# Two-layer attention and pooling trunk: buffers for the operand preparation, one more projection in block form, two clearings on ScalarE

## The chip, the cores and the metric

One core of a Trainium2 chip runs the whole program. The metric is the device time of one execution in microseconds (us), median of three runs. The engines of the core each work through their own queue in order: TensorE (PE in the profile, with its weight loads as PEld), VectorE (DVE), ScalarE (ACT), GpSimd (POOL) and SyncE (SP), which here only starts DMAs.

## The reference

A sequence of 512 tokens of 1024 channels goes through an attention layer, a feed-forward layer, a pooling layer and a second feed-forward layer. Only the attention is touched by the change:

```python
h = rmsnorm(x, attn_norm)                              # 512 x 1024
qkv = (h @ w_qkv).reshape(B, S, 3, 3, 8, 128)          # 3 groups, q/k/v, 8 heads
for g, (window, dil) in enumerate(((128, 1), (512, 4), (2048, 16))):
    outs[g], lses[g] = dilated_window_attention(q[g], k[g], v[g], window, dil, slopes[g])
o = sum(softmax(lses) * outs)                          # merged over the groups
x = x + o.reshape(512, 1024) @ w_out
```

So each of the 8 heads needs a q and a k projection in each of 3 groups (six products of 1024x128 weights with the 1024x512 normalized input), and values.

## The kernel before

**Products.** Every float32 operand is held as a high and a low part (`split`: ScalarE copies to the rounded type, VectorE subtracts), and each product takes three matmuls: high by high, high by low, low by high. A plain projection (`Product`) has 8 pieces of 128 channels, 24 matmuls of 512 columns. A pair of projections, q and k of one group, can instead be done in block form (`seven`): seven half-size products instead of eight, 84 matmuls of 256 columns, with sums of operand blocks prepared on VectorE. Head 0 is done plainly; so are the first `NSOLO = 3` groups of head 1, which is all of that head; from head 2 on all pairs go through `seven`.

**Operand preparation.** The block form needs the normalized input and its block sums. `prepare(k)` makes them for channel pieces k and k+4, for k = 0 to 3: `normed` writes the normalized pieces to one buffer h (L574, two instructions of 512 columns) and the block sums to a buffer t (L578, L579, L583), and four `split` calls (ACT L91, DVE L92) turn them into the tiles that the matmuls read (`near`, `h`, `tx`). Before, h and t are taken from the ring `raw` of four buffers, into which the weights are loaded by DMA before they are split.

**Weights.** `loads` and `steps` are queues of weight transfers and weight splits. `pump` is called behind each product and issues what has free buffers: `raw` (4), `rawhalf` (2), `w` (5), `half` (2). A plain projection takes one `raw`. A block-form pair (`Pair`) takes two `raw` and one `rawhalf`, its second buffer gets an accumulating DMA from GpSimd's queue (L172), and two additions on VectorE (L188, L189) make its third matrix.

**Order.** The Python code gives instructions in program order, and a scheduler of the framework then sets the order of each engine's queue, by its own estimate of when operands are ready. What stands in a queue is therefore not the order of the code.

**Steps around the change**, in the order of TensorE's queue:

- head 0: six plain projections, two plain value products; between them `scores0(0)` (L712), `scores12(0)` (L732, L736) and `turn_values(0)`, whose eight transposes (L685) read the two tiles `vt` that VectorE evacuates (L606): four transposes for the first tile, four for the second;
- head 1: six plain projections, evacuated by L606 to the tiles `qk`. Behind the first group's pair stands `merge(0)`: its first instruction is a matmul (L765) of `far`, which `scatter` writes on VectorE (L753) from the maxima and sums `st` of head 0. These come from `scores12(0)`: L739 and L742, L743 on VectorE, then four exponentials with their sums on ScalarE (L746). Behind the third group stand `turn0(0)` and `turn12(0)` (transposes L795, L816), then `scores0(1)` (L712);
- `values12` (L628 to L630) and, from there on, block form for everything of the attention.

`turn0` and `turn12` clear their tiles `t0` and `t12` once, by a memset on VectorE (L791, L812). These tiles lie in the room of `late` and `late12`, parts of the operand that the plain projections read.

Of the kernel before, what the change touches and what calls it, by code (L numbers as in the profile page):

```python
# [8 lines left out]
F32 = mybir.dt.float32  # L9
F32R = mybir.dt.float32r  # L10
AF = mybir.ActivationFunctionType
# [4 lines left out]
P = 128  # L16
S = 512
# [7 lines left out]
NT = S // P  # L25
# [13 lines left out]
K2 = KC // 2  # L39
NPLAIN = 4  # L40
WARM = 5
NSOLO = 3
PARTS = ((0, 2, False), (2, 10, True), (10, 18, True), (18, 22, False))
ENDS = 5
BACK = {"blocks": 3, "sums": 7}
# [19 lines left out]
def trunk(ctx: ExitStack, tc: tile.TileContext, xT, xN, norms, w_first, w_qk, w_qkp, w_v0, w_v0p, w_v12, w_out, w_pair, w_down, w_dblock, w_pin, w_pgrp,  # L65
          consts, ident_in, invcnt_in, outT, outR):
    nc = tc.nc
# [5 lines left out]
    def x_tile(k, name="x", dtype=F32):  # L73
        return cpool.tile([P, S], dtype, tag=f"x{k}", name=name)
# [4 lines left out]
    ones = cpool.tile([P, 1], F32, name="ones")  # L79
    nhalf = cpool.tile([P, NT], F32, name="nhalf")  # L80

    def ps():
        return psum.tile([P, S], F32, tag="ps", name="ps")
# [6 lines left out]
    def split(hi, lo, v):  # L90
        nc.scalar.activation(hi, v, AF.Copy)  # L91
        nc.vector.tensor_tensor(lo, v, hi.bitcast(F32), op=OP.subtract)  # L92
# [7 lines left out]
    class Held:  # L100


        def __init__(self, ring, shift=0):
            self.live = True
            n = COLS[ring]
            if ring in ("w", "half"):
                t = wpool.tile([P, 2 * n + LINE], F32R, tag=ring, name=ring, bufs=BUFS[ring])
                self.t = [t[:, shift + i * n:shift + (i + 1) * n] for i in range(2)]
            else:
                self.t = wpool.tile([P, n], F32, tag=ring, name=ring, bufs=BUFS[ring])  # L110
            rings[ring].append(self)
# [106 lines left out]
    def pairs(*srcs, shift=LINE // 4, back=False):  # L218

        these = [Pair(src, shift, back) for src in srcs]  # L220
        for parts in zip(*(p.steps() for p in these)):
            steps.extend(parts)
        units.append((these,))
# [11 lines left out]
    def plain(*srcs, lean=False):  # L235
        for src in srcs:
            share(1, src, lean=lean)

    for h in range(HEADS):
        if h == 0:  # L240
            plain(*[w_qk[u] for u in range(len(QK) - NF)])
        for g in range(3):
            if h == 1 and g < NSOLO:
                plain(*[w_qk[len(QK) - NF + 2 * g + c] for c in range(2)])
            elif h:
                pairs(w_qkp[3 * h - 3 - NSOLO + g])
        if h == 0:
# [86 lines left out]
    room, taken = {}, {}  # L334
# [36 lines left out]
    def product(layer):  # L371
        return Product(KC, stream(layer)).add(range(KC)).p
# [59 lines left out]
    def finish(lead, layer, ks):  # L432

        for f in lead:
            f.add(ks)
        r = rstd([acc[layer]])
        lead += begin(1, layer, range(4))
        row = row_of(spread(r))
        lead[-1].add(range(4, KC))
        return row  # L440
# [129 lines left out]
    def normed(layer, k, row, h, t, chained=False):  # L570

        for i in range(2):
            c = k + i * K2
            nc.vector.scalar_tensor_tensor(h.t[:, i * S:(i + 1) * S], X[c], nrm[:, layer, c:c + 1], row,  # L574
                                           op0=OP.mult, op1=OP.mult)
        hq = h.t.rearrange("p (a b c) -> p a b c", a=2, b=2)
        tq = t.t.rearrange("p (a b c) -> p a b c", a=2, b=2)
        nc.vector.tensor_sub(tq[:, :, 0], hq[:, :, 1], hq[:, 0])  # L578
        nc.vector.tensor_sub(t.t[:, H2:S], t.t[:, :H2], h.t[:, 3 * H2:])  # L579
        if chained:  # L580
            nc.vector.scalar_tensor_tensor(t.t[:, 3 * H2:], t.t[:, H2:S], -1.0, h.t[:, S:3 * H2], op0=OP.mult, op1=OP.subtract)
        else:
            nc.vector.tensor_add(t.t[:, 3 * H2:], t.t[:, H2:S], h.t[:, S:3 * H2])  # L583
        return h, t

    def halves_of(hi, lo):
        return [tuple(v[:, a * H2:(a + 1) * H2] for v in (hi, lo)) for a in range(2)]
# [8 lines left out]
    with tc.tile_pool(name="opool", bufs=1) as opool:  # L596
        early = opool.tile([P, HEADS, S], F32R, tag="o", name="early")
        with tc.tile_pool(name="apool", bufs=1) as apool:
            const = apool.tile([P, 5 * P], F32, name="const")
            d0, d12, swap = const[:, :2 * G], (const[:, 2 * G:2 * G + P], const[:, 2 * G + P:3 * G]), const[:, 3 * G:3 * G + P]  # L600
            rows = {}
# [87 lines left out]
            def blk(t, b, n=1):  # L689
                return t[:, b * P:(b + n) * P]  # L690
# [66 lines left out]
            def merge(h):  # L757
# [22 lines left out]
                for r in range(NT):  # L780
                    v = s12[:, r]
                    nc.scalar.activation(v, v, AF.Copy, scale=co[:, 1, r:r + 1])

            T0 = []

            def turn0(h):

                s0 = A[h]["s0"]
                if not T0:
                    T0.append(apool.tile([P, 2 * NT - 1, P], F32, name="t0"))  # L790
                    nc.vector.memset(T0[0], 0.0)  # L791
                own, before = T0[0][:, :NT], T0[0][:, NT:]
                p = ps()
                for b in range(NT):
                    nc.tensor.transpose(blk(p, b), s0[:, b, :P], ident)  # L795
                pb = p.rearrange("p (b q) -> p b q", b=NT)
                for j in range(NT):
                    c = slice(j * NI, (j + 1) * NI)
                    nc.scalar.copy(before[c, :, :c.stop], pb[c, 1:, :c.stop])
                    if j < NT - 1:  # L800
                        nc.scalar.copy(own[c, :, c.stop:], pb[c, :, c.stop:])
                    nc.vector.transpose(own[c, :, c], s0[c, :, P:])
                A[h]["t0"] = own, before

            T12 = []

            def turn12(h):

                s12 = A[h]["s12"]
                if not T12:  # L810
                    T12.append(apool.tile([P, 2, NT, P], F32, name="t12"))
                    nc.vector.memset(T12[0][:, 1], 0.0)  # L812
                t12 = T12[0]
                p = ps()
                for r in range(NT):
                    nc.tensor.transpose(blk(p, r), s12[:, r, :P], ident)  # L816
                nc.scalar.copy(t12[:, 0].rearrange("p r k -> p (r k)"), p)

                for j in range(NT):
                    c = slice(j * NI, (j + 1) * NI)  # L820
                    nc.vector.transpose(t12[c, 1, :, c], s12[c, :, P:])
                A[h]["t12"] = t12
# [28 lines left out]
                 + [(late12[:, 0], late12[:, 1]), tuple(late)])  # L851
            H, T, o = {}, {}, []

            def prepare(k):

                h, t = normed(0, k, rows["row"], Held("raw"), Held("raw"))
                for i in range(2):
                    held["h", k + i * K2], b = slot("h")
                    H[k + i * K2] = b[:, 0], b[:, 1]
                    split(*H[k + i * K2], h.t[:, i * S:(i + 1) * S])  # L860
                T["11", k] = halves_of(*H[k])[0]
                T["21", k], T["22", k] = halves_of(*H[k + K2])
                for i, names in enumerate((("1", "2"), ("3", "4"))):
                    if k < 2:
                        held["t", k, i], b = slot("t")
                        b = b[:, 0], b[:, 1]
                    else:
                        c = k - 2 + 2 * i
                        b = x_tile(c, "tx", F32R), x_tile(c + K2, "tx", F32R)
                    split(*b, t.t[:, i * S:(i + 1) * S])  # L870
                    for name, v in zip(names, halves_of(*b)):
                        T[name, k] = v
                h.done()
                t.done()

            OP2 = {}
# [53 lines left out]
            def later(f, *a):  # L930
                return lambda: f(*a)

            def between(h, g):

                if g == 0:
                    return {1: [later(merge, h - 1)], 3: [later(turn_values, h - 1)] if h > 1 else []} if h % 2 else {
                        1: [later(output, h - 2)], 2: [later(merge, h - 1)]}
                if g == (2 if h == 1 else 1):
                    return {0: [later(turn0, h - 1)], 2 + h % 2: [later(turn12, h - 1)], 4: [later(scores0, h)]}
                return {} if h % 2 else {2: [later(output, h - 1)]}  # L940

# [10 lines left out]
            for c in range(2):  # L952
                p = product(0)
# [7 lines left out]
            for h in range(1, HEADS):  # L961
                for g in range(3):
                    if h == 1 and g < NSOLO:
                        for c in range(2):
# [58 lines left out]
    with tc.tile_pool(name="fpool", bufs=2) as fpool:  # L1023
# [191 lines left out]
        row = finish(lead, 1, [KC - 1])  # L1215
# [4 lines left out]
        for i in (1, 0):  # L1220
            raw = Held("raw")
# [7 lines left out]
        row = finish(lead, 2, range(KC - 2, KC))  # L1229
# [67 lines left out]
        row = finish(lead, 3, range(2))  # L1297
# [53 lines left out]
        def total(t, sq):  # L1351
            new = ftile("total", H2)
            nc.vector.tensor_add(new, t, sq)
            return new

        t, late = (acc[4][:, cols] for cols in halves)
        for i in range(ENDS):
            sq = add(i, 0, end(i, 0, range(HALF)))
            if i < ENDS - 1:
                t = total(t, sq)  # L1360
        f = end(0, 1, range(HALF))
        r = rstd([t, sq])
        t = total(late, add(0, 1, f))
        t = total(t, add(1, 1, end(1, 1, range(HALF))))
# [5 lines left out]
        t = total(t, add(2, 1, end(2, 1, range(HALF // 2, HALF), f)))  # L1370
# [3 lines left out]
        t = total(t, add(3, 1, f))  # L1374
# [6 lines left out]
        r = rstd([t, sq])  # L1381
# [94 lines left out]
```

## Time and profile before

| | |
|---|---|
| three runs | 1188.02, 1188.19 (median), 1188.8 us |
| profiled execution | 1188.52 us, of which the profile's span is 1186.5 us |
| TensorE busy | 1179.0 us, 99% |
| VectorE busy | 965.5 us, 81% |
| ScalarE busy | 711.5 us, 60% |
| GpSimd busy | 173.2 us, 15% |
| granted TensorE clock | 0.999 of full speed |

The span is the time from the first to the last profiled instruction; the remaining 2 us are start and end of the execution. Matmuls overlap in time, so their recorded lengths add up to more than the time that they take: what a matmul costs is read from the distance between starts. The other engines' instructions overlap a little too.

### The profile page before, as it was taken

To read this page: it belongs to the slowest core of one execution; us is meant where nothing else is said; L and a number is where in the kernel's file an instruction comes from. 1 tells how busy PE (TensorE), PEld (TensorE's weight loads), DVE (VectorE), ACT (ScalarE), POOL (GpSimd) and SP (SyncE) were. 2 spreads that over 40 slices of the span, in tenths; PEclk is the share of its full clock that TensorE was granted. 3 is DMA by queue.
4 is the path that set the end of the run, shared out by engine and by line. 5 is a ranking of instruction groups with operands and counts; after the bars stand their busy time and mean duration, and the time that the engine had idled before them with its cause. 6 is when DMAs were issued, how large, how long until landed. Compare 5 with 4: busy or idle time off the path is not lost.

```text
span 1186.5 us, 24872 instructions
## 1 busy us (share of the span) xinstructions
PE 1179.0 (99%) x9934; PEld 1118.2 (94%) x9934; DVE 965.5 (81%) x1693; ACT 711.5 (60%) x1243; POOL 173.2 (15%) x170
## 2 busy tenths in 40 slices
PE   9999999999999999999999999999999999999997
PEld 7889999999999988889999999988889999999997
DVE  7978898889789855699988997656879998898875
ACT  6445564455455546647756775775575776676553
POOL 1111211111111002311111111122130111111100
PEclk9999999999999999999999999999999999999999
DMA  8346666665766538857777777798695777777732
GB/s 296 113 101 162 155 155 161 171 159 144 198 143 164 157 136 211 195 107 192 196 193 190 191 191 204 196 266 210 124 195 112 192 194 196 199 193 190 199 93 71
DMA packets 82003, 205.18 MB, mean 173 GB/s; under 512 B 7760, under 2 KB 13024, under 8 KB 81888
## 3 DMA queue, kind: packets, MB, share of 16 engines
q1 hardware_dynamic: 51088, 141.96, 36.3%
q0 software_dynamic: 30512, 61.36, 31.3%
q8 instruction: 77, 1.26, 0.4%
q14 instruction: 38, 0.31, 0.1%
q10 hardware_dynamic: 288, 0.29, 0.1%
HBM read 201.48 MB, written 2.10 MB: 172 GB/s over the span
## 4 chain that ended last, share of the span: by engine, by line
PE 99%; issue 1%; DVE 0%; POOL 0%; DVEq 0%; POOLq 0%
PE ps L457 20%; PE ps L459 20%; PE ps L458 20%; PE ps L325 9%; PE ps L328 8%; PE ps L326 8%; PE ps L628 2%; PE ps L630 2%; PE ps L629 2%; PE ps L918 2%; PE ps L840 1%; PE ps L712 1%; PE ps L732 1%; PE ps L834 1%; PE ps L833 0%
## 5 line engine op out<-in xcount | busy, mean ns | idle before, releaser
L91 ACT ACTIVATE w<-raw 128x1024 fp32r<-128x1024 f32 x265 | 280.6, 1063 | 175.0 <-PE ps L459 72.1
L92 DVE TENSOR_TENSOR w<-raw,w 128x1024 fp32r<-128x1024 f32 x265 | 323.0, 1222 | 47.2 <-ACT w L91 43.2
L457 PE MATMUL ps<-far,w 128*128 128x256 f32 x896 | 246.5, 275 | 0.0
L458 PE MATMUL ps<-far,w 128*128 128x256 f32 x896 | 246.5, 275 | 0.0
L459 PE MATMUL ps<-far,w 128*128 128x256 f32 x896 | 246.4, 275 | 0.0
L457 PE MATMUL ps<-near,w 128*128 128x256 f32 x640 | 180.2, 282 | 0.0
L458 PE MATMUL ps<-near,w 128*128 128x256 f32 x640 | 176.9, 276 | 0.0
L459 PE MATMUL ps<-near,w 128*128 128x256 f32 x640 | 176.8, 276 | 0.0
L457 PEld LDWEIGHTS ps<-far,w 128*128 128x128 f32 x896 | 168.2, 188 | 0.1
L458 PEld LDWEIGHTS ps<-far,w 128*128 128x128 f32 x896 | 168.2, 188 | 0.1
L459 PEld LDWEIGHTS ps<-far,w 128*128 128x128 f32 x896 | 168.2, 188 | 0.0
L325 PE MATMUL ps<-near,w 128*128 128x512 f32 (+1 forms) x332 | 125.6, 379 | 0.0
L328 PE MATMUL ps<-near,w 128*128 128x512 f32 (+1 forms) x332 | 124.9, 376 | 0.0
L326 PE MATMUL ps<-near,w 128*128 128x512 f32 (+1 forms) x332 | 124.9, 376 | 0.0
L457 PEld LDWEIGHTS ps<-near,w 128*128 128x128 f32 x640 | 120.3, 188 | 0.4
L458 PEld LDWEIGHTS ps<-near,w 128*128 128x128 f32 x640 | 120.3, 188 | 0.0
L459 PEld LDWEIGHTS ps<-near,w 128*128 128x128 f32 x640 | 120.3, 188 | 0.0
L172 POOL DMA_DIRECT2D raw<-w_pair x36 | 43.5, 1210 | 292.7 <-DMA raw<-w_pair 132.9
L325 PEld LDWEIGHTS ps<-near,w 128*128 128x128 f32 x332 | 62.3, 188 | 11.6 <-ACT near L91 0.4
L328 PEld LDWEIGHTS ps<-near,w 128*128 128x128 f32 x332 | 62.3, 188 | 11.5
L326 PEld LDWEIGHTS ps<-near,w 128*128 128x128 f32 x332 | 62.4, 188 | 11.4 <-DVE near L92 0.2
L91 ACT ACTIVATE half<-rawhalf 128x512 fp32r<-128x512 f32 x81 | 51.0, 631 | 13.9 <-PE ps L459 11.7
(310 smaller groups left out, 2763.1 us busy)
## 6 DMA issues: line engine op xcount, KB each, us to landing
raw<-w_pair SPq DMA_DIRECT2D x80, 512.0 KB, 5.0
raw<-w_qkp SPq DMA_DIRECT2D x36, 512.0 KB, 4.2
raw<-w_pair POOLq DMA_DIRECT2D x36, 512.0 KB, 7.6
raw<-w_dblock SPq DMA_DIRECT2D x32, 512.0 KB, 4.6
raw<-w_v SPq DMA_DIRECT2D x18, 512.0 KB, 4.4
raw<-w_qkp POOLq DMA_DIRECT2D x18, 512.0 KB, 7.4
rawhalf<-w_pair SPq DMA_DIRECT2D x36, 256.0 KB, 5.1
raw<-w_dblock POOLq DMA_DIRECT2D x16, 512.0 KB, 7.3
```

The costliest lines, as they stand in the source:

```text
L91: nc.scalar.activation(hi, v, AF.Copy)
L92: nc.vector.tensor_tensor(lo, v, hi.bitcast(F32), op=OP.subtract)
L172: nc.gpsimd.dma_start(self.b.rearrange("p (a c) -> p a c", a=2), self.src[:, None, 3 * n:].to_broadcast([P, 2, n]), accum_op=OP.add)
L325: nc.tensor.matmul(self.p[:, cols], w[0][:, s], mh[:, cols], start=self.done == 0, stop=False)
L326: nc.tensor.matmul(self.p[:, cols], w[0][:, s], ml[:, cols], start=False, stop=False)
L328: nc.tensor.matmul(self.p[:, cols], w[1][:, s], mh[:, cols], start=False, stop=self.done == self.n)
L457: nc.tensor.matmul(dst, w.t[0][:, c], th, start=k == 0 and not on, stop=False, skip_group_check=on)
L458: nc.tensor.matmul(dst, w.t[0][:, c], tl, start=False, stop=False, skip_group_check=on)
L459: nc.tensor.matmul(dst, w.t[1][:, c], th, start=False, stop=k == n - 1, skip_group_check=on)
L628: nc.tensor.matmul(o, mh, wh, start=k == 0, stop=False)
L629: nc.tensor.matmul(o, mh, wl, start=False, stop=False)
L630: nc.tensor.matmul(o, ml, wh, start=False, stop=k == K2 - 1)
```

## The change

`prepare` takes h from a new tile `room` (one buffer of 1024 columns, made anew for each k) and t from a free slot of the operand tiles (`Temp`), so that no buffer of the ring `raw` is taken. `NSOLO` is 2, so that the third group of head 1 is a block-form pair and its weights come as a `Pair`. The steps that stood behind that group, `turn0(0)`, `turn12(0)` and `scores0(1)`, stand between its seven products, behind the fourth, the sixth and the seventh. The two clearings are ScalarE activations (a copy of ones times 0.0).

```diff
-NSOLO = 3
+NSOLO = 2
...
+            def zero(t, n):
+                nc.scalar.activation(t, ones.to_broadcast([P, n]), AF.Copy, scale=0.0)
...
-                    nc.vector.memset(T0[0], 0.0)
+                    zero(T0[0].rearrange("p b k -> p (b k)"), (2 * NT - 1) * P)
...
-                    nc.vector.memset(T12[0][:, 1], 0.0)
+                    zero(T12[0][:, 1].rearrange("p r k -> p (r k)"), S)
...
+            class Room:
+                def __init__(self):
+                    self.t = apool.tile([P, 2 * S], F32, name="room")
+
             def prepare(k):
 
-                h, t = normed(0, k, rows["row"], Held("raw"), Held("raw"))
+                h, t = normed(0, k, rows["row"], Room(), Temp())
...
-                h.done()
                 t.done()
...
-                if g == (2 if h == 1 else 1):
+                if h == 1 and g:
+                    return {3: [later(turn0, 0)], 5: [later(turn12, 0)], 6: [later(scores0, 1)]} if g == 2 else {}
+                if g == 1:
                     return {0: [later(turn0, h - 1)], 2 + h % 2: [later(turn12, h - 1)], 4: [later(scores0, h)]}
```

The scheduler answers this with another order on VectorE. The rows of VectorE's queue from the scores of head 0 (`s0`) to the evacuation of the second value tile are, before:

```order
L715 SCALAR_TENSOR_TENSOR s0_493<-ps_494,b0_486 128x480
L715 SCALAR_TENSOR_TENSOR s0_493<-ps_529,b0_486 128x160
L606 TENSOR_TENSOR vt_445<-ps_447,row_338 128x16x16x2
L718 TENSOR_REDUCE st_491<-s0_493 128x4
L719 TENSOR_SCALAR nm_492<-st_491 128x4
L606 TENSOR_TENSOR vt_446<-ps_568,row_338 128x16x16x2
```

and after the change:

```order
L715 SCALAR_TENSOR_TENSOR s0_496<-ps_497,b0_489 128x480
L715 SCALAR_TENSOR_TENSOR s0_496<-ps_532,b0_489 128x160
L606 TENSOR_TENSOR vt_452<-ps_454,row_338 128x16x16x2
L718 TENSOR_REDUCE st_494<-s0_496 128x4
L574 SCALAR_TENSOR_TENSOR room_552<-x_69,nrm_75,row_338 128x512
L719 TENSOR_SCALAR nm_495<-st_494 128x4
L574 SCALAR_TENSOR_TENSOR room_552<-x_73,nrm_75,row_338 128x512
L92 TENSOR_TENSOR half_726<-rawhalf_423,half_726 128x512
L578 TENSOR_TENSOR temp_553<-room_552 128x2x256
L92 TENSOR_TENSOR near_82<-room_552,near_82 128x512
L579 TENSOR_TENSOR temp_553<-temp_553,room_552 128x256
L606 TENSOR_TENSOR vt_453<-ps_571,row_338 128x16x16x2
```

Six instructions, five of `prepare(2)` and one weight split, now stand ahead of the second `vt`.

The rows around `far` (L753), where `s12` are the scores of head 0's other two groups and `qk00`, `qk01` the first two projections of head 1, are before:

```order
L742 TENSOR_REDUCE st_491<-s12_617 128x4
L92 TENSOR_TENSOR near_82<-raw_549,near_82 128x512 x2
L743 TENSOR_SCALAR nm_492<-st_491 128x4
L606 TENSOR_TENSOR qk00_698<-ps_663,row_338 128x16x16x2
L753 TENSOR_TENSOR far_661<-st_491,place_443 128x64
L92 TENSOR_TENSOR w_695<-raw_474,w_695 128x1024
L578 TENSOR_TENSOR raw_550<-raw_549 128x2x256
```

and after the change:

```order
L92 TENSOR_TENSOR tx_613<-temp_601,tx_612 128x512
L92 TENSOR_TENSOR tx_617<-temp_601,tx_616 128x512
L742 TENSOR_REDUCE st_494<-s12_620 128x4
L92 TENSOR_TENSOR w_691<-raw_422,w_691 128x1024
L743 TENSOR_SCALAR nm_495<-st_494 128x4
L606 TENSOR_TENSOR qk00_694<-ps_666,row_338 128x16x16x2
L188 TENSOR_TENSOR raw_421<-raw_421,raw_422 128x512
L606 TENSOR_TENSOR qk01_729<-ps_696,row_338 128x16x16x2
L753 TENSOR_TENSOR far_664<-st_494,place_450 128x64
```

All of `prepare(2)` and `prepare(3)` (the `tx` rows are its last) and the evacuation of `qk01` now stand ahead of `far`; before, most of `prepare(2)` and all of `prepare(3)` stood behind it. TensorE's queue is the same in both programs as far as the third group of head 1: the matmul L765, which reads `far`, stands directly behind the last matmul of `qk01`. From the scores of head 1 on, the queues of all engines have the same order as before.

## The prediction

> **What bounds the kernel now.** I read the busy table first, then the chain of waits that ended last, then TensorE's own waits.
>
> ```profile
> PE 1179.0 (99%) x9934; PEld 1118.2 (94%) x9934; DVE 965.5 (81%) x1693; ACT 711.5 (60%) x1243; POOL 173.2 (15%) x170
> PE 99%; issue 1%; DVE 0%; POOL 0%; DVEq 0%; POOLq 0%
> PE ps L898 <- DVE idle L895: 1.2, 1, 1.2
> ```
>
> TensorE is on the chain for 99% of the span. The third line is the whole answer on whom TensorE waits for: once, for 1.2 us, before the first matmul. So whatever the change saves or adds on TensorE's queue goes into the time in full, and no slack behind it can take up a delay. VectorE, with 81%, is next, and it is the engine whose queue the change reorders.
>
> **Block form of head 1's third group: a gain.** From TensorE's timeline, the start of the third group, the first transpose behind it and the first matmul of `values12`; then a block-form pair of head 2 that has the same three steps between its products, with its first matmul, the steps and the first matmul of the next pair:
>
> ```profile
> 77.33 0.39 PE L325 MATMUL ps<-early,w 128*128 128x512 f32 x1
> ...
> 88.22 0.60 PE L795 MATMUL ps<-ident,s 128*128 128x128 f32 x4
> ...
> 90.48 0.39 PE L628 MATMUL ps<-w,near 128*128 128x256 f32 x1
> ...
> 124.45 0.28 PE L457 MATMUL ps<-near,w 128*128 128x256 f32 x1
> ...
> 125.82 0.60 PE L795 MATMUL ps<-ident,s 128*128 128x128 f32 x4
> ...
> 129.00 0.60 PE L816 MATMUL ps<-ident,s 128*128 128x128 f32 x4
> ...
> 132.35 1.36 PE L712 MATMUL ps<-qk,qk 128*32 128x32 f32 x88
> ...
> 136.50 0.28 PE L457 MATMUL ps<-near,w 128*128 128x256 f32 x1
> ```
>
> The plain pair takes 88.22 - 77.33 = 10.89 us and with its steps 90.48 - 77.33 = 13.15. The block-form pair with the same steps takes 136.50 - 124.45 = 12.05. Gain: 1.10 us, if its operands and weights are there.
>
> **Operand preparation outside the ring: a loss, by order.** `prepare` does the same arithmetic as before. But the weight ring no longer holds it back, so the scheduler puts `prepare(2)` and `prepare(3)` earlier in VectorE's queue, ahead of two results that TensorE reads. When TensorE reached those two points before, and when VectorE had them:
>
> ```profile
> 54.39 1.09 PE L685 MATMUL ps<-ident,vt 128*128 128x128 f32 x8
> 55.24 0.48 PE L325 MATMUL ps<-early,w 128*128 128x512 f32 x1
> ...
> 66.22 0.33 PE L765 MATMUL ps<-far,const 128*128 128x64 f32 x2
> ```
>
> ```profile
> 53.37 0.69 DVE L606 TENSOR_TENSOR vt<-ps,row 128x512 f32<-128x512 f32 x1
> ...
> 61.58 0.22 DVE L753 TENSOR_TENSOR far<-st,place 128x64 f32<-128x64 f32 x1
> ```
>
> The second `vt` was done at 54.06, and the second four of the eight transposes L685 began near 54.39 + 0.85/2 = 54.8. `far` was done at 61.8, 4.4 us ahead of L765.
>
> Now VectorE's queue after. Its rows before give the step from one start to the next where they follow without idle time:
>
> ```profile
> 41.96 1.23 DVE L92 TENSOR_TENSOR w<-raw,w 128x1024 fp32r<-128x1024 f32 x1
> 43.10 1.29 DVE L92 TENSOR_TENSOR near<-raw,near 128x512 fp32r<-128x512 f32 x2
> 44.30 1.41 DVE L574 SCALAR_TENSOR_TENSOR raw<-x,nrm,row 128x512 f32<-128x512 f32 x2
> 45.63 0.68 DVE L92 TENSOR_TENSOR half<-rawhalf,half 128x512 fp32r<-128x512 f32 x1
> 46.23 0.68 DVE L578 TENSOR_TENSOR raw<-raw 128x512 f32<-128x512 f32 x1
> ...
> 47.44 0.41 DVE L579 TENSOR_TENSOR raw<-raw 128x256 f32<-128x256 f32 x1
> 47.77 0.68 DVE L92 TENSOR_TENSOR near<-raw,near 128x512 fp32r<-128x512 f32 x1
> ...
> 51.05 0.88 DVE L715 SCALAR_TENSOR_TENSOR s<-ps,b 128x480 f32<-128x480 f32 x2
> 51.85 0.68 DVE L606 TENSOR_TENSOR vt<-ps,row 128x512 f32<-128x512 f32 x1
> ...
> 55.91 0.28 DVE L739 SCALAR_TENSOR_TENSOR s<-ps,b 128x128 f32<-128x128 f32 x1
> 56.12 1.41 DVE L574 SCALAR_TENSOR_TENSOR raw<-x,nrm,row 128x512 f32<-128x512 f32 x2
> 57.44 0.81 DVE L742 TENSOR_REDUCE st<-s 128x4 f32<-128x640 f32 x1
> 58.17 1.28 DVE L92 TENSOR_TENSOR near<-raw,near 128x512 fp32r<-128x512 f32 x2
> 59.37 0.16 DVE L743 TENSOR_SCALAR nm<-st 128x4 f32<-128x4 f32 x1
> 60.97 0.69 DVE L606 TENSOR_TENSOR qk<-ps,row 128x512 f32<-128x512 f32 x1 [1.44 <-PE ps L328]
> ```
>
> That is 1.14 for 1024 columns (41.96 to 43.10), 0.60 for 512 (45.63 to 46.23), 0.67 for one of L574 (44.30 to 45.63 for two), 0.33 for 256 (47.44 to 47.77), 0.80 for the pair L715, 0.21 for the short L739, 0.73 for a reduction (57.44 to 58.17).
>
> The anchor is the weight split at 41.96. It waits for TensorE to leave a `w` buffer, in both programs, and VectorE's queue after the change reaches it by then as well: it has one `half` split less ahead of it (0.60) and one L574 more (0.67). From this split to the second `vt` the queue after the change has 2 of 1024 columns (this one included), 11 of 512, 3 of L574, 3 of 256, one L715 pair, a reduction and a small L719 (0.1): 2.28 + 6.60 + 2.01 + 0.99 + 0.80 + 0.73 + 0.10 = 13.5 us. So the second `vt` starts at 55.5 and is done at 56.2, against 54.8 when TensorE wants it: a stall of 1.4 us.
>
> From there to `far` there are 2 of 1024, 13 of 512 (that `vt`, `n21` and the like, `qk00`, L188, `qk01`), 2 of L574, 3 of 256, the short L739, a reduction, and L743 (0.16): 2.28 + 7.80 + 1.34 + 0.99 + 0.21 + 0.73 + 0.16 = 13.5 us. `far` starts at 69.0 and is done at 69.2. Beside it runs ScalarE's part: `far` needs the four exponentials behind L743, which take 61.33 - 59.56 = 1.77 us:
>
> ```profile
> 59.56 0.43 ACT L746 ACTIVATE s<-s,nm 128x160 f32<-128x160 f32 x1 [1.38 <-DVE nm L743]
> ...
> 61.14 0.18 ACT L746 ACTIVATION_READ_ACCUMULATOR s<-s,nm 128x1 f32 x1
> ```
>
> Between L743 and `far` VectorE has three instructions of 512 columns, 1.8 us: the two come out together, so neither hides a delay of the other. I add 0.2 us for single waits on ScalarE's half of a split: `far` at 69.4. TensorE reached L765 at 66.22. The first stall only moves a part of this ahead, so the two stalls together are 69.4 - 66.22 = 3.2 us: 1.4 at L685, 1.8 at L765. I add 0.1 for one restart, since a first matmul behind other work takes about 0.1 more than the next ones. Loss: 3.3 us.
>
> Behind L765 VectorE gets its time back: TensorE is 3.3 us later, and the `prepare` instructions that stood there before are done.
>
> **Clearings, transfers, waits behind the group.** The memsets leave VectorE, which was not waited for there:
>
> ```profile
> 87.87 0.48 DVE L812 MEMSET t<- 128x512 f32 x1 [2.23 <-PE ps L328]
> ...
> 89.25 0.81 DVE L791 MEMSET t<- 128x896 f32 x1
> ```
>
> They still wait for the last plain product, which reads their room, now on ScalarE; behind them in its queue stand a weight split and the copy of the first block product. VectorE's first transpose into `t12` waits for that and holds up what is behind it, the evacuation of `qk11` and later those of the block products. TensorE needs the last of these for L736 behind the first product of `values12`. I count some 3 us of slack there: VectorE ends that evacuation about 0.8 us after the seventh product, and TensorE has `scores0(1)` and 24 matmuls of `values12` before it. So 0; without this cover up to 3 us. The pair's transfers (two of 512 KB, one of 256 KB, one accumulating) start once the weight splits around 41 us have freed buffers of the ring, against a use near 80: 0.
>
> GpSimd's bias for head 1 (L698) moves behind two accumulating DMAs in its queue, and so into the stretch on which the stalls hang. What VectorE loses beside such an instruction:
>
> ```profile
> 16.68 2.00 POOL L698 TENSOR_SCALAR b<-const 128x320 f32<-128x320 f32 x1 [16.24 <-DMA const<-consts]
> ...
> 74.31 1.35 POOL L701 TENSOR_SCALAR b<-const 128x128 f32<-128x128 f32 x2 [17.05 <-DVE st L770]
> ```
>
> ```profile
> 15.86 0.74 DVE L390 SCALAR_TENSOR_TENSOR early<-x,nrm,early 128x512 fp32r<-128x512 f32 x1
> ...
> 17.73 0.93 DVE L390 SCALAR_TENSOR_TENSOR early<-x,nrm,early 128x512 fp32r<-128x512 f32 x1
> ...
> 74.82 0.68 DVE L189 TENSOR_TENSOR raw<-raw 128x512 f32<-128x512 f32 x1
> ```
>
> L390 took 0.93 us beside it against 0.74 just ahead, L189 its usual 0.68: 0 to 0.2 us, and I take 0. The Trainium skill ("SBUF — State Buffer", Who interferes with whom) has VectorE and GpSimd share a port pair as an exclusive lock, so that a VectorE instruction with two SBUF inputs, begun second, waits out GpSimd's whole instruction. By that rule the sum would be up to 1 us higher; L189, with two such inputs, ran beside L701 without any delay, so the trace does not bear it out.
>
> **Sum.** -1.1 + 3.3 = +2.2 us. The profiled execution would go from 1188.52 to 1190.7, the median from 1188.19 to 1190.4. A measurement of this kernel tells about 0.2% (2.4 us) from no change, so this is slower, but just inside that bound.
>
> **Rivals.**
>
> *The order costs nothing and the block form's gain is left.* If VectorE ran its queue 3 us faster than my sum, L685 and L765 would find their operands, and the time would be 1188.2 - 1.1 = 1187.1. For it: VectorE had 4.4 us in hand at `far` before, and idled 1.44 us at 60.97. Against it: my sum has no idle time left in it; it is instructions alone. It decides at 66.2: `far` must be done by then.
>
> *More waits than I count.* VectorE and ScalarE hand each split to one another, and by the same count of ScalarE's queue the halves of `tx` are ready only about 0.1 us ahead. Half a microsecond late at ScalarE's four exponentials of head 0, or GpSimd's lock, comes through in full, at L765: +1 to +2 us, 1191.4 to 1192.4, clearly slower. It decides from `far` done later than 69.7.
>
> *The wait on the clearing reaches TensorE.* If VectorE's evacuations behind the clearing come 4 us later than I place them, L736 stalls for 1 us and `values12` after it: 1191.4.
>
> *The block form doesn't start in time.* If the pair's weights or sums were late, the group would lose its 1.1 us and more: 1191.5 and up. Against it: its first split stands about 2 us behind the second `vt` in VectorE's queue, near 58, and its use is near 80.
>
> **How the numbers follow.** Forecast 60%, with 1189.4 to 1191.2 as its own range (the ScalarE waits 0 to 0.5, GpSimd 0 to 0.2, the block form 1.0 to 1.2, VectorE's steps exact to 2%, 0.5). First rival, whole or in part, 12%; second 18%; third 5%; fourth 5%. The range 1188.6 to 1192.2 takes in half of the first rival's and most of the second's cases. Slower by over 0.2% means above 1190.6: the rivals two to four, 28%, and a quarter of the forecast, 15%: 0.43. Faster by over 0.2% needs 1185.8, which no case gives: 0.03 for what I don't see. The rest, 0.54, is within the bound.
>
> **What would show it.** TensorE's waits, now one line, should show L685 or L765 waiting for VectorE, some 1.4 and 1.8 us, at 55 and 68; L765 near 69.5; the first L628 near 92.6 (90.48 + 2.2); and the group from there to the end as long as before. It is wrong if TensorE's waits show nothing new, if L765 starts before 68, or if a wait appears inside the block-form group or at L736.

## The result

The kernel after takes 1190.01 us (median of 22 runs, 1189.47 to 1191.26), the kernel before 1188.20 (22 runs, 1187.80 to 1189.26): a ratio of 1.0015, 95% interval 1.0008 to 1.0021. It is slower by 1.8 us or 0.15%: the interval leaves out 1, and the size is inside the 0.2% that the prediction takes as its bound. The profiled execution took 1190.45 us, with a span of 1188.6, against 1188.52 and 1186.5.

TensorE's line of the busy table and the chain of waits, from the page of the kernel after:

```profile
PE 1178.4 (99%) x9970; PEld 1119.2 (94%) x9970; DVE 968.0 (81%) x1697; ACT 714.4 (60%) x1248; POOL 174.0 (15%) x171
PE 96%; DVE 2%; issue 1%; ACT 0%; POOL 0%; DVEq 0%; POOLq 0%; ACTq 0%
```

TensorE is busy 0.6 us less than before although the span is 2.1 us longer, and VectorE now holds a share of the chain. TensorE's waits name the places (us in total, times, longest):

```profile
PE ps L765 <- DVE far L753: 1.6, 1, 1.6
PE ps L685 <- DVE vt L606: 1.3, 1, 1.3
PE ps L904 <- DVE idle L901: 1.2, 1, 1.2
```

The third line is the wait at the start, as before. The first two are new. Their places, then the block-form group and the first product behind it, in TensorE's timeline of the kernel after (start, duration; the bracket is the idle time ahead and who ended it):

```profile
54.41 0.66 PE L685 MATMUL ps<-ident,vt 128*128 128x128 f32 x4
56.32 0.65 PE L685 MATMUL ps<-ident,vt 128*128 128x128 f32 x4 [1.26 <-DVE vt L606]
...
69.48 0.43 PE L765 MATMUL ps<-far,const 128*128 128x64 f32 x2 [1.60 <-DVE far L753]
...
80.72 0.28 PE L457 MATMUL ps<-near,w 128*128 128x256 f32 x1
...
92.75 0.39 PE L628 MATMUL ps<-w,near 128*128 128x256 f32 x1
```

L765 stood at 66.22 and now at 69.48: 3.26 us lost. The third group of head 1 with its three steps took 13.15 and now takes 92.75 - 80.72 = 12.03. L628 is 92.75 - 90.48 = 2.27 us later than before. VectorE's side of it, from its timeline of the kernel after:

```profile
41.98 1.22 DVE L92 TENSOR_TENSOR w<-raw,w 128x1024 fp32r<-128x1024 f32 x1
...
55.58 0.69 DVE L606 TENSOR_TENSOR vt<-ps,row 128x512 f32<-128x512 f32 x1
...
67.20 0.17 DVE L743 TENSOR_SCALAR nm<-st 128x4 f32<-128x4 f32 x1
...
68.47 0.69 DVE L606 TENSOR_TENSOR qk<-ps,row 128x512 f32<-128x512 f32 x1
69.19 0.23 DVE L753 TENSOR_TENSOR far<-st,place 128x64 f32<-128x64 f32 x1
```

From the split at 41.98 to `far` at 69.19 no row carries a bracket of idle time: both results were late by the number of instructions ahead of them, but for about 0.1 us in front of `far`, where ScalarE's part ended (shown below).

### The profile page after: what moved, and what is told of

Read it like the earlier page. It is cut to its first block, busy times and chain, and to the rows that moved or that the text cites. A ratio compares the mean times of both kernels' runs of the same rounds, so it can differ in the third digit from the quotient of the medians.

```text
span 1188.6 us, 24965 instructions
## 1 busy us (share of the span) xinstructions
PE 1178.4 (99%) x9970; PEld 1119.2 (94%) x9970; DVE 968.0 (81%) x1697; ACT 714.4 (60%) x1248; POOL 174.0 (15%) x171
## 4 chain that ended last, share of the span: by engine, by line
PE 96%; DVE 2%; issue 1%; ACT 0%; POOL 0%; DVEq 0%; POOLq 0%; ACTq 0%
PE ps L457 20%; PE ps L458 20%; PE ps L459 20%; PE ps L325 8%; PE ps L328 8%; PE ps L326 7%; PE ps L628 2%; PE ps L629 2%; PE ps L630 2%; PE ps L924 2%; PE ps L843 1%; PE ps L712 1%; PE ps L837 1%; PE ps L732 1%; PE ps L836 0%
## 5 line engine op out<-in xcount | busy, mean ns | idle before, releaser
L457 PE MATMUL ps<-near,w 128*128 128x256 f32 x656 | 184.8, 282 | 0.0
L458 PE MATMUL ps<-near,w 128*128 128x256 f32 x656 | 181.3, 276 | 0.0
L459 PE MATMUL ps<-near,w 128*128 128x256 f32 x656 | 181.3, 276 | 0.0
L457 PEld LDWEIGHTS ps<-near,w 128*128 128x128 f32 x656 | 123.4, 188 | 0.4
L458 PEld LDWEIGHTS ps<-near,w 128*128 128x128 f32 x656 | 123.3, 188 | 0.0
L459 PEld LDWEIGHTS ps<-near,w 128*128 128x128 f32 x656 | 123.3, 188 | 0.0
L325 PEld LDWEIGHTS ps<-near,w 128*128 128x128 f32 x332 | 62.3, 188 | 11.6 <-ACT near L91 0.4
L328 PEld LDWEIGHTS ps<-near,w 128*128 128x128 f32 x332 | 62.3, 188 | 11.5
L326 PEld LDWEIGHTS ps<-near,w 128*128 128x128 f32 x332 | 62.5, 188 | 11.3 <-DVE near L92 0.2
```

Of the source, the lines that this page charges most:

```text
L325: nc.tensor.matmul(self.p[:, cols], w[0][:, s], mh[:, cols], start=self.done == 0, stop=False)
L326: nc.tensor.matmul(self.p[:, cols], w[0][:, s], ml[:, cols], start=False, stop=False)
L328: nc.tensor.matmul(self.p[:, cols], w[1][:, s], mh[:, cols], start=False, stop=self.done == self.n)
L457: nc.tensor.matmul(dst, w.t[0][:, c], th, start=k == 0 and not on, stop=False, skip_group_check=on)
L458: nc.tensor.matmul(dst, w.t[0][:, c], tl, start=False, stop=False, skip_group_check=on)
L459: nc.tensor.matmul(dst, w.t[1][:, c], th, start=False, stop=k == n - 1, skip_group_check=on)
```

## The experiments

The theory: two results stand too far back in VectorE's queue and cost 3.3 us; the block form gives back 1.1; the clearings are free. The rivals: the block form, the clearings or late transfers cost the time, or the two stalls only stand in for some other lateness.

There are eight. To compare what the change can touch, the table takes, beside the times, two marks in each profiled execution: the start of L407 (the sums behind the lead products; nothing is changed up to there) and of the first L628 (`values12`, behind the changed group). The column between is the time from the one mark to the other.

| kernel | median us (runs) | ratio to before, 95% | L407 | L628 | between | against before |
|---|---|---|---|---|---|---|
| before | 1188.20 (22) | | 28.17 | 90.48 | 62.31 | |
| after | 1190.01 (22) | 1.0008 to 1.0021 | 28.20 | 92.75 | 64.55 | +2.24 |
| buffers | 1191.57 (9) | 1.0017 to 1.0036 | 27.78 | 93.45 | 65.67 | +3.36 |
| block | 1193.31 (5) | 1.0030 to 1.0058 | 28.32 | 89.56 | 61.24 | -1.07 (its loss, 6.0 against after, is behind L628) |
| late23 | 1186.64 (11) | 0.9977 to 0.9995 | 27.67 | 88.91 | 61.24 | -1.07 |
| memsets | 1190.26 (11) | 1.0008 to 1.0025 | 27.73 | 92.37 | 64.64 | +2.33 |
| late3 | 1188.09 (11) | 0.9991 to 1.0009 | 27.60 | 90.31 | 62.71 | +0.40 |
| dose1 | 1193.58 (5) | 1.0033 to 1.0059 | 28.23 | 96.02 | 67.79 | +5.48 |
| dose2_late | 1186.68 (11) | 0.9980 to 0.9998 | 28.14 | 89.38 | 61.24 | -1.07 |
| solo1 | 1185.75 (11) | 0.9972 to 0.9989 | 27.88 | 88.12 | 60.24 | -2.07 |

Run beside the experiments, the kernel before took 1188.19 (buffers, block, late23, memsets) and 1188.12 (the other four).

**buffers: the preparation's own buffers alone.** On the kernel before:

```diff
+            class Room:
+                def __init__(self):
+                    self.t = apool.tile([P, 2 * S], F32, name="room")
...
-                h, t = normed(0, k, rows["row"], Held("raw"), Held("raw"))
+                h, t = normed(0, k, rows["row"], Room(), Temp())
...
-                h.done()
```

> The kernel before, with the operand preparation alone in buffers of its own (head 1's third group stays plain, the clearings stay on VectorE). My theory, that VectorE's order costs 3.3 us and the block form saves 1.1: the waits at L685 (about 1.3 us) and L765 (about 1.6 us) are there as in the kernel after, and the time is before + 3.3, about 1191.5 us (1191.2 to 1191.9), which is slower than the kernel after. Rival, the loss comes from the block form or from the clearings on ScalarE: no such waits, and the time of before, 1188.2.

Measured 1191.57, between the marks +3.36. TensorE's waits in this kernel:

```profile
PE ps L765 <- DVE far L753: 1.6, 1, 1.6
PE ps L685 <- DVE vt L606: 1.3, 1, 1.3
```

The same two waits, with no block form and no clearing on ScalarE. This part alone costs 3.4 us; what the kernel after has besides gives 1.1 back (3.36 - 2.24).

**memsets: the kernel after with the clearings back on VectorE.**

```diff
-                    zero(T0[0].rearrange("p b k -> p (b k)"), (2 * NT - 1) * P)
+                    nc.vector.memset(T0[0], 0.0)
...
-                    zero(T12[0][:, 1].rearrange("p r k -> p (r k)"), S)
+                    nc.vector.memset(T12[0][:, 1], 0.0)
```

> The kernel after, with both clearings back on VectorE. My theory takes the clearings at nothing: the time of the kernel after within 0.2 us, with the same two waits of TensorE. Rival, ScalarE's clearings hold up its queue and so the evacuations of the first block group: 0.5 us or more below the kernel after.

Measured 1190.26, between the marks 0.09 us more than the kernel after. In this kernel the clearings decide nothing, on either engine.

**late23: the kernel after with both preparations behind the scatter.**

```diff
                 scaled_by(VT[c], p, True)
-                prepare(2 + c)
             scores12(0)
             turn_values(0)
             scatter(0)
+            prepare(2)
+            prepare(3)
```

> The kernel after, with both further preparations written behind the scatter of head 0 and nothing else changed. My theory: the second vt is done before TensorE wants it and far several us ahead, so both waits go (at most 0.2 us left at L685), and the block form's gain remains: 3.3 us under the kernel after by the working, before - 1.1, about 1187.1 us (1186.8 to 1187.5). Rival, the stalls of the kernel after cover other lateness (operands of the block group, the ring's transfers), which then turns up elsewhere: about the time of before or of after, with a new wait between 70 and 95 us.

Measured 1186.64, 3.4 us under the kernel after and 1.55 under the kernel before; between the marks 3.31 under and 1.07 under. Two rows each of VectorE's timeline and of TensorE's in this kernel:

```profile
53.55 0.69 DVE L606 TENSOR_TENSOR vt<-ps,row 128x512 f32<-128x512 f32 x1
...
60.67 0.23 DVE L753 TENSOR_TENSOR far<-st,place 128x64 f32<-128x64 f32 x1
```

```profile
53.93 1.09 PE L685 MATMUL ps<-ident,vt 128*128 128x128 f32 x8
...
65.76 0.33 PE L765 MATMUL ps<-far,const 128*128 128x64 f32 x2
```

The eight transposes run in one piece again and `far` is ready 4.9 us early. Nothing was hidden behind the stalls: no other wait came in their place. The order alone is worth 3.3 us, and without it the change is a gain.

**late3: only the last preparation behind the scatter.**

```diff
-                prepare(2 + c)
+                if c == 0:
+                    prepare(2)
...
             scatter(0)
+            prepare(3)
```

> The kernel after, with only the last preparation, prepare(3), written behind the scatter of head 0. VectorE keeps prepare(2) ahead of the second vt but has six instructions of 512 columns less ahead of far. My theory, each stall from its own place in VectorE's queue: the wait at L685 stays at 1.3 us, the one at L765 goes, and the time is that of before + 1.4 - 1.1, about 1188.5 us (1188.1 to 1188.9). Rival, the two stalls are one delay that only shows at two places (a lateness common to both, such as a transfer): both shrink or both stay.

Measured 1188.09, ratio 1.0000; between the marks +0.40. TensorE's wait, VectorE's `far` and TensorE's reader of it in this kernel:

```profile
PE ps L685 <- DVE vt L606: 1.3, 1, 1.3
```

```profile
64.70 0.23 DVE L753 TENSOR_TENSOR far<-st,place 128x64 f32<-128x64 f32 x1
```

```profile
67.16 0.33 PE L765 MATMUL ps<-far,const 128*128 128x64 f32 x2
```

One stall stays whole, the other is gone: `far` is done at 64.9 against L765 at 67.16. So they are two delays with a cause each. `prepare(2)` in front of the second `vt` costs 0.40 + 1.07 = 1.47 us, `prepare(3)` in front of `far` 2.24 - 0.40 = 1.84.

**dose1: useless work ahead of `far`.** The kernel after, with head 0's first score evacuation issued twice:

```diff
-                for b, p, k in ((b12[:, :P], p, slice(0, P)), (b12[:, P:], n[:, :P], slice(P, G))):
+                for b, p, k in ((b12[:, :P], p, slice(0, P)),) * (1 if h else 2) + ((b12[:, P:], n[:, :P], slice(P, G)),):
```

> The kernel after, with the evacuation of head 0's scores (L739, 128x512) issued twice, so that VectorE has 0.6 us of useless work ahead of far; by the order L189 and a half split move ahead of far too, 0.6 us each. My theory, far is limited by VectorE's queue alone: far and L765 1.8 us later, the wait there 3.4 us instead of 1.6, and the time 1.8 us above the kernel after, if TensorE goes on at its full pitch; behind the 3.0 us wait in the kernel with the preparation in the ring it ran at half its pitch for 6 us, and if it does so here, another 3 us, 4.8 in all. Rival, far waits for something else than VectorE's queue: less than 1 us.

Measured 1193.58, 3.6 above the kernel after; between the marks 3.24 more. TensorE's timeline in this kernel, then TensorE's clock by stretch of time (the windows; the column ahead of the DMA share is the granted clock):

```profile
71.12 0.43 PE L765 MATMUL ps<-far,const 128*128 128x64 f32 x2 [3.21 <-DVE far L753]
...
72.26 0.63 PE L325 MATMUL ps<-early,w 128*128 128x512 f32 x1
72.68 0.63 PE L326 MATMUL ps<-early,w 128*128 128x512 f32 x1
```

```profile
71.80:72.00 0.20, 0.20 (x3) 0.15 (x2) 0.20 (x1) 0.00 (x0) 0.00 (x0) 1.00 0.67 266
72.00:72.20 0.20, 0.20 (x2) 0.16 (x1) 0.20 (x1) 0.00 (x0) 0.00 (x0) 0.52 0.98 236
...
72.50:75.00 2.50, 2.50 (x7) 1.91 (x7) 1.98 (x11) 0.47 (x2) 1.44 (x2) 0.50 0.58 131
...
75.40:75.60 0.20, 0.20 (x3) 0.16 (x2) 0.20 (x2) 0.20 (x2) 0.14 (x1) 0.95 1.04 430
```

The wait grew by 1.6 us, near the 1.8 of the three further instructions ahead of `far`: that is VectorE's queue. The other 1.6 us are the clock: some eight matmuls start 0.43 us apart instead of 0.23. The half pitch came as expected, but for 3.4 us rather than 6, so its price was half of what I expected.

**dose2_late: the same work where there is slack.** On late23, the line above with 3 in the place of 2.

> The kernel with both further preparations behind the scatter, with L739 (128x512) issued three times: 1.2 us of useless work on VectorE ahead of far and of all that follows. My theory: far was done near 60.9 and is wanted at 65.8, the last operand split ends near 68 and is first used in the block group at 77, so the 1.2 us disappear in this slack: the time of the kernel without them, 1186.6 us, within 0.3. Rival, VectorE's work counts wherever it stands: 1.2 us more.

Measured 1186.68, late23 1186.64; between the marks both have 61.24. VectorE's timeline in this kernel, then TensorE's:

```profile
62.34 0.23 DVE L753 TENSOR_TENSOR far<-st,place 128x64 f32<-128x64 f32 x1
...
68.55 0.69 DVE L92 TENSOR_TENSOR tx<-temp,tx 128x512 fp32r<-128x512 f32 x1
```

```profile
66.23 0.33 PE L765 MATMUL ps<-far,const 128*128 128x64 f32 x2
```

`far` is ready 3.7 us ahead of its use at 66.2 and the last operand 8 us ahead of the block group (77.34). 1.2 us of VectorE work cost nothing here, while in dose1 the extra work came through at L765: what counts is what stands ahead of a result that is waited for, not the engine's busy share.

**block: the block form without the preparation's own buffers.** The kernel after, with the ring back and the memsets of the kernel before:

```diff
-                h, t = normed(0, k, rows["row"], Room(), Temp())
+                h, t = normed(0, k, rows["row"], Held("raw"), Held("raw"))
...
+                h.done()
                 t.done()
```

> The kernel after, with the operand preparation back in the ring of raw weights (head 1's third group in block form, clearings on VectorE). VectorE has the second vt and far early again, so my theory has no waits at L685 and L765 and the full gain of the block form: before - 1.1, about 1187.1 us (1186.8 to 1187.4), if the last operands come in time. They are made behind far here, about 10 us ahead of the block group at most: if they are late, the group begins with a wait of its own and the time is up to 1190. Rival, the block form itself costs the time: slower than before with no wait at its start.

Measured 1193.31, above both times that my theory allowed, and slower than before with no wait at the group's start, which was the sign of the rival. But the rival's cause is not it: the two early waits are gone, and up to L628 the gain of the block form is there, -1.07. The loss is behind it: from L628 to the end this kernel's profiled execution takes 1193.31 - 89.56 = 1103.75 us, the kernel after 1190.45 - 92.75 = 1097.70. TensorE's waits, the clock in the windows, and ScalarE's and VectorE's rows ahead of it:

```profile
PE ps L736 <- DVE qk L511: 3.0, 1, 3.0
```

```profile
95.80:96.00 0.20, 0.00 (x0) 0.00 (x0) 0.20 (x1) 0.00 (x0) 0.00 (x0) 0.72 0.94 164
...
99.00:102.00 3.00, 3.00 (x16) 3.00 (x15) 2.34 (x6) 2.25 (x11) 1.27 (x2) 0.50 0.40 129
...
102.60:102.80 0.20, 0.20 (x3) 0.20 (x2) 0.02 (x1) 0.20 (x3) 0.00 (x0) 0.72 0.66 61
```

```profile
83.03 2.01 ACT L91 ACTIVATE w<-raw 128x1024 fp32r<-128x1024 f32 x2 [3.52 <-DMA raw<-w_v]
88.21 1.06 ACT L91 ACTIVATE w<-raw 128x1024 fp32r<-128x1024 f32 x1 [3.18 <-DMA raw<-w_v]
```

```profile
89.30 1.23 DVE L92 TENSOR_TENSOR w<-raw,w 128x1024 fp32r<-128x1024 f32 x1 [2.82 <-ACT w L91]
...
95.73 0.69 DVE L511 TENSOR_TENSOR qk<-ps,sums 128x512 f32<-128x512 f32 x1
```

ScalarE twice waits for weights, VectorE's split waits for ScalarE, and the evacuation L511 behind them in the queue is late, at 95.73 against 92.02 in the kernel after. Why the weights are late shows in SyncE's queue, first of this kernel, then of the kernel after (issues of `w_v`, the weights of the values), and in what SyncE waited for in this kernel between 60 and 95 us:

```profile
76.54 0.33 SPq L169 DMA_DIRECT2D raw<-w_v  x1
78.91 0.33 SPq L170 DMA_DIRECT2D raw<-w_v  x1
```

```profile
68.64 0.33 SPq L169 DMA_DIRECT2D raw<-w_v  x1
...
72.48 0.33 SPq L170 DMA_DIRECT2D raw<-w_v  x1
```

```profile
SPq L169 <- DVE raw L583: 18.1, 1, 18.1
...
SPq L170 <- DVE tx L92: 2.0, 1, 2.0
```

They are issued 8 and 6 us later: the ring's buffers are held by the preparation, by its sums (L583) and by its last splits (`tx`), which run until 78.9. This kernel also has the clearings on VectorE, and one of them (L815, 0.48 us at 92.39) stands in the queue ahead of L511, so up to half a microsecond of the wait may be its. Of the kernels here, then, the block form pays only in those that prepare its operands outside the ring; what costs is the place in the order that came with that. Behind the wait the half clock costs as much as the wait itself (windows above): 3.0 + about 3.0.

**solo1: one block-form group more.** On late23:

```diff
-NSOLO = 2
+NSOLO = 1
```

> The kernel with both further preparations behind the scatter, and head 1's second group in block form as well (NSOLO 1). If a block-form pair saves 1.1 us wherever its operands are there in time: 1.1 us under that kernel, about 1185.5 us. By VectorE's queue the last operand of the first product is ready near 66.2 (used 66.9), the last of the third near 68.2 (used 69.4): about 1 us of slack each, so a wait of up to 1 us, and with it no gain, is as possible. Rival, the ring's transfers for a second block group come too late: a wait of its own of several us, slower than 1187.

Measured 1185.75, 2.4 us under the kernel before and 4.3 under the kernel after; between the marks 1.00 under late23. TensorE has no wait behind the start. VectorE's timeline, then TensorE's:

```profile
65.23 0.70 DVE L92 TENSOR_TENSOR h<-room,h 128x512 fp32r<-128x512 f32 x1
...
67.65 0.70 DVE L92 TENSOR_TENSOR tx<-temp,tx 128x512 fp32r<-128x512 f32 x1
```

```profile
68.67 0.28 PE L457 MATMUL ps<-h,w 128*128 128x256 f32 x1
...
70.08 0.28 PE L457 MATMUL ps<-tx,w 128*128 128x256 f32 x1
```

The operands come 2.7 and 1.7 us ahead of their first use. The gain repeats in a second group, and this is the fastest of all the versions.

## Why the prediction held

**Block form, -1.10.** 12.03 us measured for the group with its steps, 12.05 taken from head 2's pair. The experiments give 1.07 (late23), 1.12 (after against buffers) and 1.00 for the next group (solo1). It started on time: no wait in or around the group.

**Order, +3.3 in two stalls of 1.4 and 1.8 plus 0.1.** Counted instructions put the second `vt` at 55.5 and `far` at 69.0, with 0.2 more for ScalarE; measured 55.58 and 69.19. The profile's idle times at the two places are 1.26 and 1.60, and by the experiments the stalls cost 1.47 and 1.84, restarts included; L765 stands at 69.48 against "near 69.5". That VectorE's queue and ScalarE's exponentials would come out together also held, as the last exponential in ScalarE's timeline of the kernel after shows:

```profile
68.98 0.19 ACT L746 ACTIVATION_READ_ACCUMULATOR s<-s,nm 128x1 f32 x1
```

It ended at 69.17, and VectorE's step in front of `far` (68.47 to 69.19) is 0.72 instead of 0.60. The experiments show what was only argued from the order: each stall hangs on one `prepare` and goes when it is moved, and the second grows with work put ahead of it.

**Clearings, 0.** ScalarE's two, and the slack at L736 on which this rested (ScalarE's, VectorE's and TensorE's timelines of the kernel after):

```profile
80.24 0.63 ACT L785 ACTIVATE t<-ones 128x512 f32<-128x512 f32 x1 [3.70 <-PE ps L328]
...
81.88 0.93 ACT L785 ACTIVATE t<-ones 128x896 f32<-128x896 f32 x1
```

```profile
92.62 0.41 DVE L512 TENSOR_TENSOR qk<-sums,ps 128x256 f32<-128x256 f32 x1
```

```profile
96.61 0.46 PE L736 MATMUL ps<-qk,qk 128*32 128x32 f32 x32
```

The evacuation ends at 93.0, 3.6 us ahead of L736; I had counted some 3. That this cover can run out I had as a rival. The kernel block shows it for another cause, late weights, and it then cost 6 us rather than the 1 us I gave that rival: I had not seen the clock behind such a wait.

**GpSimd, 0 of a possible 0.2.** L698 did move behind two DMAs, but it ran no later for that: at 50.98, before at 52.09. L701 ran beside a split with two SBUF inputs (GpSimd's and VectorE's timelines of the kernel after):

```profile
71.08 1.52 POOL L701 TENSOR_SCALAR b<-const 128x128 f32<-128x128 f32 x2 [19.08 <-DVE st L770]
```

```profile
71.23 1.23 DVE L92 TENSOR_TENSOR w<-raw,w 128x1024 fp32r<-128x1024 f32 x1
```

The split took 1.23 us against 1.22 elsewhere. By the exclusive lock in the Trainium skill ("SBUF — State Buffer", Who interferes with whom) it would have waited at least until the first of the two was over; this trace does not show that either.

**Sum, +2.2.** Between the marks +2.24, at L628 +2.27. The profiled execution took 1190.45 and not 1190.7, the median 1190.01 and not 1190.4. The difference lies outside the stretch that the change touches. L407, up to which no kernel differs, started anywhere from 27.60 to 28.32 in the ten profiled executions, but that scatter of the start is only 0.03 us between these two. Behind L628 they differ by 1098.04 - 1097.70 = 0.3 us, and all of it comes at the very end: the last L407 still starts 2.26 us later than before (1181.45 against 1179.19), and the rest of the execution takes 9.00 against 9.33. Why that end differs is open.

## What to carry to other kernels

Taking buffers out of a shared ring also takes away the wait that kept work back. Where a scheduler then puts that work earlier on a busy in-order engine, count what stands ahead of each result that the bound engine reads: the sum of their steps, from one start to the next, gave both stalls here to 0.1 us. If one is late, don't undo the buffers, write the freed work behind the results that are wanted sooner; and note that TensorE's waits of 1.3 and 1.6 us cost little more than themselves (1.5 and 1.8), while those of 3.0 and 3.2 us cost 6.0 and 4.8.

## What was not expected of the hardware

TensorE's clock answers to waits, and not in proportion. Around the waits of 1.3 and 1.6 us in the kernel after the granted clock stayed at 1.00, as its window shows:

```profile
54.00:80.00 26.00, 23.14 (x136) 18.88 (x136) 23.45 (x47) 13.43 (x32) 2.68 (x3) 1.00 0.41 108
```

In dose1, after 3.2 us of waiting, it fell to 0.50 only at 72.0, 0.9 us after work had begun again, and came back at 75.4; in block it fell at 95.9, within the wait of 3.0, and came back at 102.7. (The times follow from the short windows shown with the two experiments: a mean of 0.72 over 0.20 us is half speed for 0.11 of them.) So the slow stretch lasted 3.4 us in one and 6.8 in the other, for waits of nearly the same length. The Trainium skill ("TensorE: Matmul & The Clock Gate", Part 1) has TensorE's activity watched in free-running windows of about 3.4 us; that the two stretches are one such window and two is an estimate by this figure, and it fits both traces. The clock records of the traces fit it elsewhere too: the stretch at full speed ahead of the fall lasted 64.85 us in dose1 and 88.75 in block, 19 and 26 times 3.413. By the same estimate the windows at whose end the clock fell were not idle throughout: TensorE was idle in them for some 2.5 us in dose1 (68.6 to 71.1) and 2.4 in block (93.5 to 95.9). From which wait on the clock falls, between 1.6 and 3.0 us, no run here tells.

The scatter of the start goes with the clock as well. In the ten traces the clock reaches full speed between 4.31 us (late3) and 7.16 us (dose1) after the start of the span, and the start of L407 follows in nearly the same order, from 27.60 (late3) to 28.23 (dose1) and 28.32 (block, clock at 7.14). So between two executions half a microsecond and more can come from there, which is why the table compares from mark to mark.
